# Where the fourth set of activation forms is made, ahead of the seven-product feed-forward

## The chip, the core and the metric

The kernel runs on one NeuronCore of a Trainium2 chip. The metric is the device time of one launch, in microseconds (us). The engines are named as the profile names them: PE is the matmul engine (PEld its weight loads), DVE the vector engine, ACT the scalar engine, POOL the general one, SP the queue from which nearly all loads are issued. Each engine takes its own instructions in the order of the program.

## The reference

A two-layer decoder trunk runs over 512 prompt rows and 32 sample rows (8 sequences of 4), together T = 544 columns of the activation matrix, 1024 features high. Each layer is half feed-forward, mixer, half feed-forward, gated embedding. The feed-forward is what matters here, and it runs four times:

```python
def rmsnorm(x, g):
    y = x * lax.rsqrt(jnp.mean(x * x, axis=-1, keepdims=True) + EPS)
    return y * g
def swiglu(x, w1, w3, w2):
    return (jax.nn.silu(x @ w1) * (x @ w3)) @ w2
# in layer i
h = h + 0.5 * swiglu(rmsnorm(h, ffn1_norm[i]), ffn1_w1[i], ffn1_w3[i], ffn1_w2[i])
h = h + mixer(rmsnorm(h, mix_norm[i]))          # layer 0: gMLP, layer 1: attention
h = h + 0.5 * swiglu(rmsnorm(h, ffn2_norm[i]), ffn2_w1[i], ffn2_w3[i], ffn2_w2[i])
```

All is in float32; the inner width of the feed-forward is 2816.

## The kernel before

**Layout.** Features lie on the 128 partitions, so the activations h are 8 chunks of 128 x 544. A float32 product is made of three matmuls of rounded halves: each operand is split into a high part (a rounded copy, on ACT) and a low part (source less high part, on DVE), and PE adds high x high, high x low and low x high. The 544 columns are taken as two halves of 272.

**Weights.** SP loads a block of 128 x 1024 (`_load`, L208). `_sum` makes a sum or difference of two blocks on DVE (L227), and `_split` the two parts of a piece (ACT cast L241, then DVE subtraction L242). `prepare` runs these a few pieces ahead of the piece that PE takes. All of them, the activations and the forms below live in one pool of 45 buffers named `big`, each 128 x 1088 floats.

**The feed-forward** (`ffn`) has three stretches. First `plain` pairs of inner blocks are made in the plain way: per pair four tiles (two blocks, w1 and w3), each 8 x 6 matmuls (`mm`, L285, L289, L291) with one copy out of PSUM on ACT (L471). The first feed-forward of layer 0 makes two pairs (eight plain tiles), the other three make one (four). Beside the first tile, ACT and DVE also make the norm's factor `rstd` (L385 to L403).

Then `ffn_steps` makes the remaining pairs by a scheme of Strassen's kind with seven products in place of eight (L538, 24 matmuls each; order 1, 5, 6, 2, 7, 3, 4), and puts tiles of the second matrix w2 (L285 to L291, added to h at L577) between them. Products 1, 6, 7 and 4 gather in one PSUM buffer, so what stands there is read out between them: ACT copies after 1, 5 and 6 (L546), DVE adds after 2 (L553), after 7 (L555) and after 3 (L557), and ACT copies after 4 (L560). Product 4 may not start before L555 has read the buffer. There are three PSUM buffers named `ps`: two hold the sums of the products and one the tile of w2, so the next tile of w2 may not start before L577 has read the last.

The gate of a finished pair (`gate`) is four steps: times `rstd` (DVE L496), Silu (ACT L499), product (DVE L502), split (L329, L330). One step of each open pair follows each product. In `ffn_steps` the order of PE, ACT, DVE and POOL is that in which the code is written; ahead of it a list scheduler places the instructions of each engine by its own rules.

**The forms.** Products 3, 5, 6, 7 and 4 need differences of the activations. Per pair of chunks `forms` makes one set: two scaled copies on ACT (L351), then on DVE

```python
nc.vector.tensor_tensor(two(t13), x[:, :, HT:], two(x[:, 0, :]), ALU.subtract)      # L355
self.split_pair(f13, t13)                                                           # ACT L329, DVE L330
nc.vector.tensor_tensor(t24[:, :HT], x[:, 1, HT:], t13[:, :HT], ALU.subtract)       # L357
nc.vector.tensor_tensor(t24[:, HT:], x[:, 1, :HT], t24[:, :HT], ALU.subtract)       # L358
self.split_pair(f24, t24)                                                           # ACT L329, DVE L330
```

So a set is four instructions of ACT, five of DVE and three `big` buffers (x, which is free after L358, and f13 and f24, which stay for the whole feed-forward). Four sets are needed. `box["f"]` holds those that the stage ahead has made: none ahead of the first feed-forward, three ahead of the second (the mixer of layer 0 makes sets 0, 1 and 2 as chunks 1, 3 and 5 are done), two ahead of the third and two ahead of the fourth. In `ffn` the rest is made beside the plain tiles by `more(n)`, which makes one set if fewer than n are there. With one pair and fewer than three sets (`lead`) it is called ahead of each tile; otherwise after each tile's copy, with a count that grows with the tile.

Of the kernel before, what the change touches and what calls it, by code (L numbers as in the profile page):

```python
# [51 lines left out]
NKP = NC_ // 2  # L52
# [50 lines left out]
def halves(x):  # L103

    return x.rearrange("p (a b) -> p a b", a=2)
# [27 lines left out]
def whole(p):  # L133

    return unwoven(span(p))


class Builder:
# [312 lines left out]
    def ffn(self, h, box, gcol, rstd, on_chunk, plain=1):  # L451

        nc, eng = self.nc, mybir.EngineType
        self.ahead = (2, 3, 6)
        first, xs, xf = [], self.pairs(box), box["f"]

        def more(n):
            if len(xf) < min(n, NKP):
                xf.append(self.forms(h, gcol, len(xf), xs))
        hid, todo = {}, ([], [])  # L460
        lead = plain == 1 and len(xf) < 3
        for f in range(2 * plain):
            g = self.big()
            for w in range(2):
                if lead:
                    more(len(xf) + 1)
                if rstd is None:
                    p, rstd = self.tile_rstd(xs, box["acc"])
                else:
                    p = self.tile_mm(xs)  # L470
                nc.scalar.copy(halves(g[:, w]), whole(p))  # L471
                for t in todo:
                    if t:
                        t.pop(0)()
                if not lead:
                    more((2 * f + w + 1) // plain)
            first.append((f // 2, f % 2, g))
            if f % 2 and f < 2 * plain - 1 or lead and f == 0:
                for j, a, g in first:
                    todo[a].extend(self.gate(hid, rstd, j, a, g))  # L480
                first = []
        assert self.chain is None
        for j, a, g in first:
            todo[a].extend(([None] * 3 if j == 0 else []) + self.gate(hid, rstd, j, a, g))
        with self.tc.manual_schedule(engines={eng.PE, eng.Activation, eng.DVE, eng.Pool}):
            self.ffn_steps(h, xf, rstd, hid, todo, plain, on_chunk)
        self.ahead = (2, 2, 4)
        self.pins = 2
        return rstd
# [1106 lines left out]
```

## Time and profile before

| what | us |
|---|---|
| median of three timed runs | 1931.98 (1931.47 to 1932.03) |
| the profiled execution, its own time | 1931.48 |
| its span | 1929.7 |
| first feed-forward: eight plain tiles end, products begin | 56.95 |
| second feed-forward: four plain tiles end, products begin | 528.80 |

Times of rows count from the start of the span; the profiled execution lasts 1.78 us longer than it. A row of the timeline gives the start, the length, the engine, the line and operation, the tiles (written <- read) and in brackets how long the engine sat idle ahead of it and what ended that. Rows of one kind that follow each other are merged (x48). An instruction's length reaches until its result is written, so the next on the same engine can start some 0.1 us before the length is over.

### The profile page before, as it was taken

Reading aid. Unit: us, or ns where it says so; the run is one execution under the profiler, and the core shown is the slowest. Engines: PE = TensorE matmul, PEld = TensorE weight load, DVE = VectorE, ACT = ScalarE, POOL = GpSimd, SP = SyncE. Lnnn points to the kernel's source line nnn. Section 1 sums busy time; section 2 is a strip of 40 time slices with the busy share of each in tenths; the row PEclk is TensorE's granted clock in tenths of the full one; section 3 lists DMA queues with packets and bytes.
Section 4 is the critical chain, followed back from the end, with each engine's and each line's share of the span. In section 5 each row is a group of like instructions: output and inputs, shape, how many; then the busy total and the mean of one; then the engine's idle time right before and its main releaser. Section 6 shows DMA issues by size and latency. Waiting matters only on the chain.

```text
span 1929.7 us, 39007 instructions
## 1 busy us (share of the span) xinstructions
PE 1906.5 (99%) x16508; PEld 1872.2 (97%) x16508; DVE 1457.5 (76%) x1799; ACT 950.2 (49%) x1396; POOL 142.6 (7%) x190
## 2 busy tenths in 40 slices
PE   9999999999999999999999999999999999999999
PEld 8999999999999999999999999999977899999999
DVE  7887877556788877766578887877476888878774
ACT  7544434424554444454466454444374754444461
POOL 0000000410100000023000000001131300000020
PEclk9999999999999999999999999999999999999999
DMA  5233234312223233431484232324769332332431
GB/s 195 79 112 121 84 123 147 108 48 88 88 88 107 86 120 105 153 104 45 144 306 157 103 129 69 129 86 136 217 210 341 101 110 81 112 113 86 139 109 47
DMA packets 98048, 237.62 MB, mean 123 GB/s; under 512 B 12130, under 2 KB 29826, under 8 KB 97874
## 3 DMA queue, kind: packets, MB, share of 16 engines
q1 hardware_dynamic: 97730, 235.09, 36.9%
q8 instruction: 130, 2.13, 0.5%
q14 instruction: 44, 0.36, 0.1%
q10 hardware_dynamic: 144, 0.04, 0.0%
HBM read 218.65 MB, written 16.44 MB: 122 GB/s over the span
## 4 chain that ended last, share of the span: by engine, by line
PE 89%; DVE 6%; ACT 3%; issue 1%; DMA 1%; POOL 0%; SPq 0%; ACTq 0%; DVEq 0%; POOLq 0%
PE ps L538 31%; PE ps L285 15%; PE ps L291 15%; PE ps L289 15%; PE pb L538 5%; DVE big L242 2%; ACT big L241 1%; DVE big L227 1%; DMA big<-in_cv 1%; PE ps L891 1%; PE ps L892 1%; PE ps L893 1%; DVE big L496 0%; DVE big L330 0%; PE ps L1285 0%
## 5 line engine op out<-in xcount | busy, mean ns | idle before, releaser
L538 PE MATMUL ps<-big,big 128*128 128x272 f32 x5616 | 668.8, 279 | 5.9 <-DVE big L555 3.5
L538 PEld LDWEIGHTS ps<-big,big 128*128 128x128 f32 x5616 | 658.5, 189 | 7.0 <-issue 4.0
L242 DVE TENSOR_TENSOR big<-big,big 128x1024 fp32r<-128x1024 f32 (+2 forms) x505 | 582.8, 1157 | 93.4 <-ACT big L241 92.9
L241 ACT CAST big<-big 128x1024 fp32r<-128x1024 f32 (+2 forms) x505 | 483.1, 977 | 326.5 <-DVE big L227 251.9
L285 PE MATMUL ps<-big,big 128*128 128x272 f32 x2668 | 531.3, 280 | 3.8 <-ACT big L241 2.3
L291 PE MATMUL ps<-big,big 128*128 128x272 f32 x2668 | 529.2, 280 | 1.8 <-DVE big L242 1.7
L289 PE MATMUL ps<-big,big 128*128 128x272 f32 x2668 | 528.3, 279 | 0.0
L285 PEld LDWEIGHTS ps<-big,big 128*128 128x128 f32 x2668 | 408.3, 189 | 8.5 <-ACT big L241 5.7
L291 PEld LDWEIGHTS ps<-big,big 128*128 128x128 f32 x2668 | 407.9, 189 | 3.6 <-DVE big L242 3.1
L289 PEld LDWEIGHTS ps<-big,big 128*128 128x128 f32 x2668 | 407.9, 189 | 0.0
L370 POOL TENSOR_TENSOR st<-st,tmp 128x544 f32<-128x544 f32 (+1 forms) x63 | 87.5, 1389 | 1476.7 <-ACT tmp L368 1476.5
L227 DVE TENSOR_TENSOR big<-big,big 128x1024 f32<-128x1024 f32 x156 | 190.2, 1219 | 0.0
L577 DVE SCALAR_TENSOR_TENSOR big<-ps,big 128x544 f32<-128x544 f32 x128 | 92.5, 723 | 104.0 <-PE ps L291 103.0
L546 ACT COPY tmp<-ps 128x544 f32<-128x544 f32 x117 | 71.6, 612 | 107.5 <-PE ps L538 107.2
L496 DVE TENSOR_TENSOR big<-big,st 128x1088 f32<-128x1088 f32 x88 | 113.2, 1289 | 3.3 <-ACT big L560 2.0
L538 PE MATMUL pb<-big,big 128*128 128x272 f32 x936 | 114.8, 279 | 0.0
L538 PEld LDWEIGHTS pb<-big,big 128*128 128x128 f32 x936 | 111.3, 189 | 0.0
L499 ACT ACTIVATE big<-big 128x544 f32<-128x544 f32 x88 | 58.0, 660 | 88.1 <-DVE big L496 88.0
L341 ACT ACTIVATE big<-big,gains 128x544 fp32r<-128x544 f32 (+1 forms) x80 | 55.3, 703 | 90.3 <-DVE big L577 55.0
L330 DVE TENSOR_TENSOR big<-big,big 128x544 fp32r<-128x544 f32 (+1 forms) x112 | 79.4, 715 | 22.8 <-ACT big L329 22.6
L342 DVE SCALAR_TENSOR_TENSOR big<-big,gains,big 128x544 fp32r<-128x544 f32 (+1 forms) x80 | 64.6, 817 | 23.4 <-ACT big L341 23.4
L329 ACT CAST big<-big 128x544 fp32r<-128x544 f32 (+1 forms) x112 | 71.2, 644 | 11.9 <-DVE big L502 7.5
(218 smaller groups left out, 1388.5 us busy)
## 6 DMA issues: line engine op xcount, KB each, us to landing
big<-in_w SPq DMA_DIRECT2D x156, 512.0 KB
big<-in_w2b SPq DMA_DIRECT2D x96, 384.0 KB
big<-in_w13p SPq DMA_DIRECT2D x16, 512.0 KB
big<-in_w2a SPq DMA_DIRECT2D x16, 512.0 KB
big<-in_win SPq DMA_DIRECT2D x16, 512.0 KB
big<-in_wg SPq DMA_DIRECT2D x16, 512.0 KB
big<-in_ck SPq DMA_DIRECT2D x16, 512.0 KB
big<-in_cv SPq DMA_DIRECT2D x16, 512.0 KB
```

The lines of the kernel that those rows point to most:

```text
L227: self.nc.vector.tensor_tensor(t, a, b, ALU.add if op == "+" else ALU.subtract)
L241: self.nc.scalar.copy(hi, src)
L242: self.nc.vector.tensor_tensor(lo, src, hi.bitcast(F32), ALU.subtract)
L285: i = nc.tensor.matmul(o, wh, xh[:, b], start=s, stop=False)
L289: nc.tensor.matmul(o, wh, xl[:, b], start=False, stop=False)
L291: nc.tensor.matmul(o, wl, xh[:, b], start=False, stop=e)
L330: self.nc.vector.tensor_tensor(pair[:, 1, cols], src, pair[:, 0, cols].bitcast(F32), ALU.subtract)
L370: nc.gpsimd.tensor_tensor(acc[:, cols], acc[:, cols], sq, ALU.add)
L496: tt(g, g, rstd.unsqueeze(1).broadcast_to([P, 2, T]), ALU.mult)
L538: nc.tensor.matmul(turns(dst[w]), a[:, c], woven(b), start=k in "152" and kp == 0 and n == 0, stop=kp == NKP - 1 and n == 2, skip_group_ch ...
L546: nc.scalar.copy(t["r" + k], t["C" if k == "5" else "A"])
L577: nc.vector.scalar_tensor_tensor(halves(h[c]), whole(out), 0.5, halves(h[c]), ALU.mult, ALU.add)
```

## The change

One line of `ffn`, the call after each plain tile:

```diff
                 if not lead:
-                    more((2 * f + w + 1) // plain)
+                    more((2 * f + w + 1) // plain if len(xf) < 3 else NKP)
```

NKP is 4. Where three sets are there, the call asks for all four, so the fourth is made after the tile at which it stands. This touches two places. In the second feed-forward three sets are there from the start: the fourth was made after plain tile 4 and is now made after tile 1. In the first feed-forward (two pairs, counts 0, 1, 1, 2, 2, 3, 3, 4) the third set comes with tile 6, so the fourth is made after tile 7 where it was made after tile 8. The third and fourth feed-forward take the other branch (`lead`) and keep their order. PE's, POOL's and SP's instructions keep theirs as well; on SP some loads go to other buffers of the pool and so wait for other instructions.

Second feed-forward, DVE. L392 ends the norm's factor beside the first plain tile; L242 and L227 are low parts and sums of weights; L355 to L330 are the fourth set. Before, the set stands behind the low part for product 5 and the sum for product 6, ahead of the low parts for products 6 and 2 (the last two rows):

```order
L392 SCALAR_TENSOR_TENSOR st_6042<-tmp_6043,st_6042 128x544
L227 TENSOR_TENSOR big_6122<-big_6057,big_6059 128x1024
L242 TENSOR_TENSOR big_6175<-big_6122,big_6174 128x1024
L227 TENSOR_TENSOR big_6178<-big_6122,big_5987 128x1024
L355 TENSOR_TENSOR tmp_6233<-big_6230 128x544
L357 TENSOR_TENSOR tmp_6234<-big_6230,tmp_6233 128x272
L358 TENSOR_TENSOR tmp_6234<-big_6230,tmp_6234 128x272
L330 TENSOR_TENSOR big_6235<-tmp_6233,big_6235 128x544
L330 TENSOR_TENSOR big_6236<-tmp_6234,big_6236 128x544
L242 TENSOR_TENSOR big_6272<-big_6178,big_6271 128x1024
L242 TENSOR_TENSOR big_6276<-big_6061,big_6275 128x1024
```

With the change it stands among the steps of the norm's factor, ahead of the low part of the fourth plain tile's weights (the last row):

```order
L403 TENSOR_TENSOR tmp_6033<-st_5502,tmp_6032 128x544
L355 TENSOR_TENSOR tmp_6056<-big_6053 128x544
L357 TENSOR_TENSOR tmp_6057<-big_6053,tmp_6056 128x272
L388 SCALAR_TENSOR_TENSOR tmp_6043<-st_6042 128x544
L358 TENSOR_TENSOR tmp_6057<-big_6053,tmp_6057 128x272
L330 TENSOR_TENSOR big_6058<-tmp_6056,big_6058 128x544
L391 SCALAR_TENSOR_TENSOR tmp_6043<-pb_6036,tmp_6043 128x272
L391 SCALAR_TENSOR_TENSOR tmp_6043<-pb_6037,tmp_6043 128x272
L330 TENSOR_TENSOR big_6059<-tmp_6057,big_6059 128x544
L392 SCALAR_TENSOR_TENSOR st_6042<-tmp_6043,st_6042 128x544
L242 TENSOR_TENSOR big_6068<-big_5924,big_6067 128x1024
```

and behind the sum for product 6 (second L227 of the next piece) the low parts for products 6 and 2 come at once:

```order
L242 TENSOR_TENSOR big_6133<-big_5987,big_6132 128x1024
L227 TENSOR_TENSOR big_6136<-big_6071,big_6073 128x1024
L242 TENSOR_TENSOR big_6189<-big_6136,big_6188 128x1024
L227 TENSOR_TENSOR big_6192<-big_6136,big_5987 128x1024
L242 TENSOR_TENSOR big_6272<-big_6192,big_6271 128x1024
L242 TENSOR_TENSOR big_6276<-big_6075,big_6275 128x1024
```

The five instructions of DVE moved up by six to nine places.

Second feed-forward, ACT. L471 are the copies of the four plain tiles, L351 and L329 the fourth set, L241 high parts of weights, L546 the first copies out of the products. Before:

```order
L241 CAST big_6118<-big_5987 128x1024
L471 COPY big_5982<-ps_6067 128x544
L471 COPY big_6117<-ps_6124 128x544
L241 CAST big_6174<-big_6122 128x1024
L351 ACTIVATE big_6230<-big_95,gains 128x544 x2
L329 CAST big_6235<-tmp_6233 128x544
L471 COPY big_6117<-ps_6180 128x544
L329 CAST big_6236<-tmp_6234 128x544
L241 CAST big_6271<-big_6178 128x1024
L241 CAST big_6275<-big_6061 128x1024
L546 COPY tmp_6308<-ps_6246 128x544
```

With the change, from the copy of the first plain tile on:

```order
L471 COPY big_5982<-ps_5989 128x544
L351 ACTIVATE big_6053<-big_95,gains 128x544 x2
L385 ACTIVATE st_6042<-pb_6036,eps 128x272
L385 ACTIVATE st_6042<-pb_6037,eps 128x272
L329 CAST big_6058<-tmp_6056 128x544
L329 CAST big_6059<-tmp_6057 128x544
L241 CAST big_6067<-big_5924 128x1024
L471 COPY big_5982<-ps_6081 128x544
L241 CAST big_6132<-big_5987 128x1024
L471 COPY big_6131<-ps_6138 128x544
L241 CAST big_6188<-big_6136 128x1024
L241 CAST big_6271<-big_6192 128x1024
```

The four instructions of the set moved to behind the first L471; the cast of the fourth plain tile's weights (first L241 of the piece) stands behind them, that of product 1's weights behind the second L471, and those for products 6 and 2 ahead of the last L471.

First feed-forward, ACT, from the copy of plain tile 7 to the first copy out of the products. Before:

```order
L471 COPY big_592<-ps_601 128x544
L241 CAST big_653<-big_597 128x1024
L329 CAST big_709<-big_175 128x544
L329 CAST big_712<-big_328 128x544
L351 ACTIVATE big_715<-big_95,gains 128x544 x2
L471 COPY big_592<-ps_659 128x544
L329 CAST big_720<-tmp_718 128x544
L329 CAST big_721<-tmp_719 128x544
L241 CAST big_758<-big_657 128x1024
L241 CAST big_762<-big_524 128x1024
L546 COPY tmp_791<-ps_731 128x544
```

With the change:

```order
L471 COPY big_592<-ps_601 128x544
L351 ACTIVATE big_653<-big_95,gains 128x544 x2
L329 CAST big_658<-tmp_656 128x544
L329 CAST big_659<-tmp_657 128x544
L241 CAST big_667<-big_597 128x1024
L329 CAST big_723<-big_175 128x544
L329 CAST big_726<-big_328 128x544
L471 COPY big_592<-ps_673 128x544
L241 CAST big_758<-big_671 128x1024
L241 CAST big_762<-big_524 128x1024
L546 COPY tmp_791<-ps_731 128x544
```

The set now stands ahead of the cast for product 5 (first L241) and ahead of the copy of tile 8 (second L471), where it stood behind both. On DVE it moved in the same way: from behind the low part for product 5, the sum for product 6 and the splits of the first gated pair to ahead of them.

## The prediction

> **What bounds the kernel now.** I read the page's busy times first, then its chain, then PE's waits.
>
> ```profile
> span 1929.7 us, 39007 instructions
> PE 1906.5 (99%) x16508; PEld 1872.2 (97%) x16508; DVE 1457.5 (76%) x1799; ACT 950.2 (49%) x1396; POOL 142.6 (7%) x190
> PE 89%; DVE 6%; ACT 3%; issue 1%; DMA 1%; POOL 0%; SPq 0%; ACTq 0%; DVEq 0%; POOLq 0%
> ```
>
> PE works 1906.5 of 1929.7 us and holds 89% of the chain; the change leaves its work alone. So the change can win only from the 23.2 us in which PE stands still, and it can lose only by making PE wait anew. PE's waits by releaser:
>
> ```profile
> PE ps L538 <- DVE big L555: 3.5, 3, 2.1
> PE ps L538 <- ACT tmp L546: 2.4, 3, 1.3
> PE ps L285 <- DVE big L577: 1.4, 2, 0.7
> ```
>
> The first three numbers of the list are the total, the count and the longest. Which of them lie in the two feed-forwards that the change touches, the timeline of PE shows. Second feed-forward:
>
> ```profile
> 528.80 8.50 PE L538 MATMUL ps<-big,big 128*128 128x272 f32 x72
> 537.14 2.94 PE L538 MATMUL pb<-big,big 128*128 128x272 f32 x24
> 539.92 5.72 PE L538 MATMUL ps<-big,big 128*128 128x272 f32 x48
> 547.79 11.36 PE L538 MATMUL ps<-big,big 128*128 128x272 f32 x96 [2.14 <-DVE big L555]
> ...
> 564.54 2.94 PE L538 MATMUL ps<-big,big 128*128 128x272 f32 x24
> ...
> 568.22 0.47 PE L285 MATMUL ps<-big,big 128*128 128x272 f32 x2 [0.74 <-DVE big L577]
> ```
>
> These are products 1, 5, 6, then 2, then 7 and 3, then 4 and the next pair's. One product takes 539.92 - 537.14 = 2.78 us. Products 7 and 3 would let product 4 begin at 539.92 + 5.56 = 545.48; it begins at 547.79, so 2.31 us are lost (the row says 2.14, since it counts from the modelled end). Likewise 568.22 - 564.54 - 2.78 = 0.90 us are lost at L577. First feed-forward:
>
> ```profile
> 56.95 5.72 PE L538 MATMUL ps<-big,big 128*128 128x272 f32 x48
> 63.32 3.05 PE L538 MATMUL ps<-big,big 128*128 128x272 f32 x24 [0.64 <-ACT tmp L546]
> ...
> 71.76 2.94 PE L538 MATMUL ps<-big,big 128*128 128x272 f32 x24
> 75.34 0.47 PE L285 MATMUL ps<-big,big 128*128 128x272 f32 x2 [0.63 <-DVE big L577]
> ```
>
> Lost: 63.32 - 62.51 = 0.81 us ahead of product 6, and 75.34 - 74.54 = 0.80 us at L577. The four together are 4.82 us; this is all that the change can reach.
>
> **The change, second feed-forward.** DVE around the fourth set:
>
> ```profile
> 525.09 1.23 DVE L242 TENSOR_TENSOR big<-big,big 128x1024 fp32r<-128x1024 f32 x1 [5.92 <-ACT big L241]
> 526.23 1.22 DVE L227 TENSOR_TENSOR big<-big,big 128x1024 f32<-128x1024 f32 x1
> 527.37 0.72 DVE L355 TENSOR_TENSOR tmp<-big 128x544 f32<-128x544 f32 x1
> ...
> 531.14 2.36 DVE L242 TENSOR_TENSOR big<-big,big 128x1024 fp32r<-128x1024 f32 x2 [0.22 <-ACT big L241]
> 533.41 1.22 DVE L227 TENSOR_TENSOR big<-big,big 128x1024 f32<-128x1024 f32 x1
> 535.75 1.23 DVE L242 TENSOR_TENSOR big<-big,big 128x1024 fp32r<-128x1024 f32 x1 [1.11 <-ACT big L241]
> ...
> 539.28 1.23 DVE L242 TENSOR_TENSOR big<-big,big 128x1024 fp32r<-128x1024 f32 x1 [1.17 <-ACT big L241]
> 540.42 2.49 DVE L496 TENSOR_TENSOR big<-big,st 128x1088 f32<-128x1088 f32 x2
> ...
> 543.96 0.78 DVE L553 TENSOR_TENSOR big<-pb,tmp 128x272 f32<-128x272 f32 x2
> 544.65 1.22 DVE L242 TENSOR_TENSOR big<-big,big 128x1024 fp32r<-128x1024 f32 x1
> ...
> 546.92 0.72 DVE L555 TENSOR_TENSOR big<-ps,tmp 128x544 f32<-128x544 f32 x1
> ...
> 567.36 0.72 DVE L577 SCALAR_TENSOR_TENSOR big<-ps,big 128x544 f32<-128x544 f32 x1
> ```
>
> The set costs DVE 531.14 - 527.37 = 3.77 us, with its own waits, just as the products begin. From there to L555 DVE never waits for PE: it is late by itself, and L555, whose product 7 was done at 539.92 + 2.78 = 542.70, runs at 546.92. With the change the set falls into the 5.92 us in which DVE had nothing to do (up to 525.09). That idle time is its cover. The weights of plain tile 4 then stand behind it. A plain tile has 48 pairs of matmuls like two products, so 5.56 us; tile 1 ends near 528.80 - 3 x 5.56 = 512.1, its copy takes 0.6, the two scaled copies of the set 1.4 (an estimate from the copy's length), the set on DVE 3.8, the last steps of the norm's factor between them up to 2 (four of the same size), the low part of the tile's weights 1.2: done between 519.1 and 521.1, and I take 519.8, since ACT and DVE overlap. Tile 4 begins at 528.80 - 5.56 = 523.24. So 2.1 to 4.1 us of cover are left; each us beyond that would cost one.
>
> What is late next? The chain sum L227, ACT cast, low part L242 takes 535.75 - 533.41 = 2.34 us. ACT's rows matter now too:
>
> ```profile
> 529.00 0.61 ACT L471 COPY big<-ps 128x544 f32<-128x544 f32 x1 [0.23 <-PE ps L291]
> ...
> 538.20 1.05 ACT L241 CAST big<-big 128x1024 fp32r<-128x1024 f32 x1 [1.97 <-DVE big L227]
> 539.15 0.61 ACT L546 COPY tmp<-ps 128x544 f32<-128x544 f32 x1
> ...
> 542.02 0.66 ACT L499 ACTIVATE big<-big 128x544 f32<-128x544 f32 x1
> 542.94 0.66 ACT L499 ACTIVATE big<-big 128x544 f32<-128x544 f32 x1 [0.26 <-DVE big L496]
> 543.50 1.03 ACT L241 CAST big<-big 128x1024 fp32r<-128x1024 f32 x1
> ```
>
> - Low parts for 6 and 2: 526.23 + 2.34 = 528.57 (was 531.14). Sum for 7: + 2.27 (533.41 - 531.14) = 530.84.
> - Its cast now finds ACT at the copy after product 1. A copy starts 0.20 us after PE's next work does (529.00 against 528.80), so at 531.78; the cast follows 0.50 later (539.15 to about 539.65) at 532.28, its low part 1.08 later (538.20 to 539.28) at 533.36, the sum for 3 at 534.50 (1.14 later, as 539.28 to 540.42), its low part at 536.84, L496 at 537.98, L553 at 541.52 (3.54 later).
> - ACT's copy after product 6 cannot precede 537.14 + 0.20 = 537.34 (was 539.15). From it to the cast at 543.50 are 4.35 us, less 0.36 by which the second L499 was held (542.02 to 542.94 is 0.92, the next pitch 0.56): 541.33. Its low part comes at 542.41, later than DVE would be ready (541.52 + 0.69), so ACT decides: 2.24 us ahead of 544.65.
> - L555 follows 2.27 later, at 544.68, and PE 0.87 after it (546.92 to 547.79), at 545.55. Of the 2.31 us, 0.07 remain.
>
> Between L555 and L577 DVE runs without a wait for PE, so L577 also comes 2.24 earlier and PE's start there moves from 568.22 to 565.98. **Second feed-forward: 2.24 us.** Later PE and DVE go on with the same distance as before.
>
> **First feed-forward.**
>
> ```profile
> 51.59 0.61 ACT L471 COPY big<-ps 128x544 f32<-128x544 f32 x1 [2.00 <-PE ps L291]
> ...
> 62.66 0.60 ACT L546 COPY tmp<-ps 128x544 f32<-128x544 f32 x1
> ```
>
> ```profile
> 65.52 1.22 DVE L227 TENSOR_TENSOR big<-big,big 128x1024 f32<-128x1024 f32 x1
> ...
> 74.47 0.72 DVE L577 SCALAR_TENSOR_TENSOR big<-ps,big 128x544 f32<-128x544 f32 x1
> ```
>
> Here DVE has no large gap and the set moves by one tile. ACT makes the scaled copies behind the copy at 51.59 (0.5 and 1.4, until 53.5), DVE the set in about 3.4 (3.77 above, of which a part was waiting for ACT) until 56.9, then the low part for 5 (1.14; product 5 needs it at 56.95 + 2.78 = 59.73, so 1.7 us of cover) and the sum for 6, done at 59.2. ACT then casts twice (1.0 each) and copies at 61.2, where it stood at 62.66: before, both casts stood behind the set's last split. PE starts 0.66 after that copy (62.66 to 63.32), so it could at 61.9, ahead of 62.51: the 0.81 us go. What is late next is the low part for product 6, which I get done at 62.8, when PE wants it at 62.51 + 0.46; up to 0.2 us may remain. Behind ACT's copy (0.5) stand two Silus (0.56 each) and a cast whose low part follows 1.08 later, at 63.9; it is of half size (0.6), so the sum at 65.52 comes at 64.48. From there to L577 it is DVE with ACT, not PE: L577 comes 1.04 earlier and PE from 75.34 to 74.30. **First feed-forward: 1.04 us**, whatever remains at product 6, since L577 decides.
>
> **The sum** is 3.3 us: 1931.48 - 3.3 = 1928.2 for the profiled execution, and 1928.7 against the median of 1931.98, which lies 0.5 above it. Unknown are the new waits of loads and the places where I put an instruction between rows. Their bounds are 4.82 us won (all four waits gone: 1927.2) and, below, the case in which the waits only move.
>
> [...] The change takes two lasting buffers some 14 us sooner, so loads behind it get other buffers. The three loads of the next blocks, and the answer on who waited for a load between 485 and 600:
>
> ```profile
> 500.49 1.28 SPq L208 DMA_DIRECT2D big<-in_w  x3
> ```
>
> ```profile
>   ACT big L241: 0.2, 1
> ```
>
> They were issued from 500.49 on; they now wait for buffers that PE reads up to the first three k-steps of the mixer's last tile, 0.7 us apart, so they go some 1 us later. The sum that reads the first two stands at about 520.9. From issue to use there are 19 us, and nothing but 0.2 us ever waited for a load here. I take 0 and keep 0.2 us as the other end. [...]
>
> **The rivals.**
>
> *All four waits go*: if DVE comes 1 us earlier still at both L577, PE never waits there: 4.8 us, 1927.2. For it speaks that DVE's waits for ACT shrink; against, that the copy after product 6 cannot precede PE.
>
> *The waits move*: L555 comes early, but a copy after a product (L546) or L577 holds PE in its place, in one feed-forward or both. The three waits for L546 of up to 1.3 us show that this happens. About half is given back: 1.0 to 2.0 us won, 1930.0 to 1931.0.
>
> *Slower*: DVE and ACT take the set in order, so a load that lands late would hold the sum at 520.9 and all that stands behind. It decides once that sum begins later than 525.09 - 2.34 = 522.75: then the low part at 525.09 is late, and so is L555. From there each us takes one from the win of 3.3, and slower by 0.2% needs a landing near 530: 1936. The 19 us speak against it.
>
> *It does nothing*: were the gap up to 525.09 filled by other work first, the set would end as late as now: 1932. The order shows the set ahead of the second copy, so this is unlikely.
>
> **How the numbers follow.** The forecast has 0.60, all four gone 0.19, the waits move 0.14, slower 0.04, nothing 0.03. Predicted is 1928.7. The range goes from 1927.2 to 1931.0, which leaves out little but the last two cases. A time counts as faster from 0.2% on, 3.86 us below 1931.98, about what a measurement of this kernel can tell from no change: that is under 1928.1. The forecast lies 0.6 us above that bound; 0.08 of its 0.60 may fall below. With the 0.19 that makes faster 0.27; slower is 0.04 and within 0.2% the other 0.69.
>
> **What would show it.** In the profile of the changed kernel DVE should have L355 near 514 and no set behind 526; L555 should stand near 544.7 less the 1.0 that the first feed-forward gives, the wait ahead of product 4 should be under 0.3, the wait for L546 ahead of the first feed-forward's product 6 gone, and both waits for L577 still there with 0.5 to 0.8 us lost. I am wrong if L555 still holds PE by over 0.5 us, if PE waits for a low part (L242) in the plain tiles, or if a sum (L227) waits for a load.

## The result, and the profile after

| | before | changed |
|---|---|---|
| median of 14 runs each, on one chip, us | 1931.34 (1930.51 to 1932.29) | 1927.2 (1926.71 to 1928.32) |
| ratio, 95% interval | | 0.998 (0.9973 to 0.9987) |
| the profiled execution, its own time | 1931.48 | 1928.06 |
| its span | 1929.7 | 1926.3 |

The change makes the kernel 4.1 us faster (1931.34 - 1927.2; by the interval 2.5 to 5.2). The page of the changed kernel, its first lines and the chain:

```profile
span 1926.3 us, 39008 instructions
PE 1904.8 (99%) x16508; PEld 1869.8 (97%) x16508; DVE 1457.4 (76%) x1799; ACT 949.2 (49%) x1396; POOL 143.4 (7%) x190
PE 89%; DVE 5%; ACT 2%; DMA 2%; issue 1%; SPq 0%; POOL 0%; ACTq 0%; DVEq 0%
```

Each engine listed has as many instructions as before, and PE's share of the chain is the same. The waits of PE (total, count, longest) show where the time went:

```profile
PE ps L538 <- ACT tmp L546: 1.7, 2, 1.3
PE ps L538 <- DVE big L555: 1.4, 2, 1.0
PE ps L285 <- DVE big L577: 1.2, 2, 0.7
```

Of three waits for L555 the one of 2.1 us is gone (3.5 to 1.4), of three for L546 one of 0.7 (2.4 to 1.7); both for L577 are still there. PE's timeline, first feed-forward and then second:

```profile
56.21 8.55 PE L538 MATMUL ps<-big,big 128*128 128x272 f32 x72
64.60 2.94 PE L538 MATMUL pb<-big,big 128*128 128x272 f32 x24
70.16 2.94 PE L538 MATMUL ps<-big,big 128*128 128x272 f32 x24
73.59 0.47 PE L285 MATMUL ps<-big,big 128*128 128x272 f32 x2 [0.48 <-DVE big L577]
...
527.05 8.50 PE L538 MATMUL ps<-big,big 128*128 128x272 f32 x72
535.39 2.94 PE L538 MATMUL pb<-big,big 128*128 128x272 f32 x24
538.17 16.96 PE L538 MATMUL ps<-big,big 128*128 128x272 f32 x144
...
560.53 2.94 PE L538 MATMUL ps<-big,big 128*128 128x272 f32 x24
564.20 0.47 PE L285 MATMUL ps<-big,big 128*128 128x272 f32 x2 [0.73 <-DVE big L577]
```

Products 1, 5 and 6 of the first feed-forward now run as one row (x72), and so do products 7, 3, 4 and the next pair's first three in the second (x144): nothing holds PE inside. To compare kernels I take two stretches, each from the start of product 1 to PE's start behind the first L577. The first went from 75.34 - 56.95 = 18.39 to 73.59 - 56.21 = 17.38 us, the second from 568.22 - 528.80 = 39.42 to 564.20 - 527.05 = 37.15 us. That is 1.01 + 2.27 = 3.28 us. Between them lie 453.46 us in both kernels (528.80 - 75.34 and 527.05 - 73.59). DVE in the second feed-forward:

```profile
512.09 0.72 DVE L355 TENSOR_TENSOR tmp<-big 128x544 f32<-128x544 f32 x1 [2.22 <-ACT big L351]
...
516.79 2.36 DVE L242 TENSOR_TENSOR big<-big,big 128x1024 fp32r<-128x1024 f32 x2
519.07 1.22 DVE L227 TENSOR_TENSOR big<-big,big 128x1024 f32<-128x1024 f32 x1
523.28 1.23 DVE L242 TENSOR_TENSOR big<-big,big 128x1024 fp32r<-128x1024 f32 x1 [2.99 <-ACT big L241]
524.42 1.22 DVE L227 TENSOR_TENSOR big<-big,big 128x1024 f32<-128x1024 f32 x1
526.75 2.36 DVE L242 TENSOR_TENSOR big<-big,big 128x1024 fp32r<-128x1024 f32 x2 [1.11 <-ACT big L241]
...
542.91 0.72 DVE L555 TENSOR_TENSOR big<-ps,tmp 128x544 f32<-128x544 f32 x1
```

The set stands at 512.09, its idle stretch has shrunk from 5.92 to 2.99 us, and behind the sum at 524.42 there is no L355 any more.

### The profile page after: what moved, and what is told of

Read it like the earlier page. It is cut to its first block, busy times and chain, and to the rows that moved or that the text cites. A ratio compares the mean times of both kernels' runs of the same rounds, so it can differ in the third digit from the quotient of the medians.

```text
span 1926.3 us, 39008 instructions
## 1 busy us (share of the span) xinstructions
PE 1904.8 (99%) x16508; PEld 1869.8 (97%) x16508; DVE 1457.4 (76%) x1799; ACT 949.2 (49%) x1396; POOL 143.4 (7%) x190
## 4 chain that ended last, share of the span: by engine, by line
PE 89%; DVE 5%; ACT 2%; DMA 2%; issue 1%; SPq 0%; POOL 0%; ACTq 0%; DVEq 0%
PE ps L538 31%; PE ps L285 15%; PE ps L291 15%; PE ps L289 15%; PE pb L538 5%; DVE big L242 1%; DMA tmp<-rows 1%; ACT big L241 1%; PE ps L891 1%; PE ps L892 1%; PE ps L893 1%; DVE big L227 1%; DVE big L330 0%; PE ps L1285 0%; PE ps L676 0%
## 5 line engine op out<-in xcount | busy, mean ns | idle before, releaser
L242 DVE TENSOR_TENSOR big<-big,big 128x1024 fp32r<-128x1024 f32 (+2 forms) x505 | 582.1, 1156 | 86.7 <-ACT big L241 85.9
L241 ACT CAST big<-big 128x1024 fp32r<-128x1024 f32 (+2 forms) x505 | 482.4, 975 | 325.1 <-DVE big L227 251.5
L227 DVE TENSOR_TENSOR big<-big,big 128x1024 f32<-128x1024 f32 x156 | 190.1, 1219 | 0.0
L577 DVE SCALAR_TENSOR_TENSOR big<-ps,big 128x544 f32<-128x544 f32 x128 | 92.5, 722 | 104.1 <-PE ps L291 103.2
L546 ACT COPY tmp<-ps 128x544 f32<-128x544 f32 x117 | 71.5, 611 | 111.3 <-PE ps L538 111.3
L330 DVE TENSOR_TENSOR big<-big,big 128x544 fp32r<-128x544 f32 (+1 forms) x112 | 79.3, 714 | 22.7 <-ACT big L329 22.5
L329 ACT CAST big<-big 128x544 fp32r<-128x544 f32 (+1 forms) x112 | 71.2, 643 | 12.2 <-DVE big L502 7.4
```

Source lines behind the costliest of these rows:

```text
L227: self.nc.vector.tensor_tensor(t, a, b, ALU.add if op == "+" else ALU.subtract)
L241: self.nc.scalar.copy(hi, src)
L242: self.nc.vector.tensor_tensor(lo, src, hi.bitcast(F32), ALU.subtract)
L330: self.nc.vector.tensor_tensor(pair[:, 1, cols], src, pair[:, 0, cols].bitcast(F32), ALU.subtract)
L546: nc.scalar.copy(t["r" + k], t["C" if k == "5" else "A"])
L577: nc.vector.scalar_tensor_tensor(halves(h[c]), whole(out), 0.5, halves(h[c]), ALU.mult, ALU.add)
```

## The experiments

The theory: the set of forms costs the path what DVE and ACT spend on it, if it stands beside the products, and nothing if it falls into DVE's idle stretch. The rivals: the buffers and loads that move with it are what counts; each tile sooner gives its share; part of the cost has only moved. All edits are to the line of the change, except in the last one.

**Each feed-forward alone.** First the second one:

```diff
-                    more((2 * f + w + 1) // plain if len(xf) < 3 else NKP)
+                    more((2 * f + w + 1) // plain if len(xf) < 3 or plain == 2 else NKP)
```

> Only the second feed-forward has its fourth set after plain tile 1; the first keeps the order of before. I measure two stretches: S1, from the start of product 1 of the first feed-forward to PE's start behind the first L577 (before 75.34 - 56.95 = 18.39 us, after 73.59 - 56.21 = 17.38), and S2, the same in the second (before 568.22 - 528.80 = 39.42, after 564.20 - 527.05 = 37.15). Theory (each place pays by itself, because DVE's queue is shorter by one set when the products begin): S1 18.39, S2 37.15, both within 0.1, and the time 2.3 us below before. Rival (the second place only pays because the first moved the buffers of the pool): S2 stays at 39.4. Rival (the rest of the measured 4.1 us comes from the start of the program, where product 1 began 0.74 us sooner): the products begin at 56.2 here too, though the order up to there is that of before; by the theory that start only varies from run to run.

and then the first one (`or plain == 1`):

> Only the first feed-forward has its fourth set one tile sooner; the second keeps the order of before. Theory: S1 17.38 and S2 39.42, both within 0.1, the time 1.0 us below before. Rival (PE's wait for L577 there would have shrunk by itself): S1 18.4. If both parts were worth half of 4.1, the time would be 2.0 below before.

Measured: with the second alone 1927.49 us against 1930.93 (ratio 0.9983, 0.9974 to 0.9992), stretches 73.89 - 55.44 = 18.45 and 564.52 - 527.36 = 37.16. With the first alone 1929.69 us against 1930.93 (0.9993, 0.9984 to 1.0002), stretches 73.21 - 55.81 = 17.40 and 566.08 - 526.66 = 39.42. Each half gives its own stretch what the whole change gives it and leaves the other as before. The interval of the first alone takes in 1, so its gain is read from the stretch. By the stretches the two gains are independent, and the second feed-forward carries two thirds. The times fell by more than was expected of them: 1930.93 - 1927.49 = 3.44 us with the second alone, where 2.3 was expected, and 1.24 us with the first alone, where 1.0 was.

**The set one and two tiles later** (second feed-forward, first as with the change; `f + w > 0` and `f > 0`):

```diff
-                    more((2 * f + w + 1) // plain if len(xf) < 3 else NKP)
+                    more((2 * f + w + 1) // plain if len(xf) < 3 else NKP if plain == 2 or f > 0 else 0)
```

> The fourth set of the second feed-forward is made with plain tile 2, one tile later than the change makes it; the first feed-forward is as with the change. Theory (all that counts is whether the set falls into the stretch in which DVE has nothing to do, which ends when the low part of the weights for product 1 is due): the set still falls into it, so 37.15 us from product 1's start to PE's start behind the first L577, within 0.2, and no wait of PE for L555 over 0.3. Rival (each tile later gives back its share of the 3.4 us between the placings with tile 1 and with tile 3): 38 to 39 us, with a wait for L555 between 0.8 and 1.5.

> The second feed-forward makes its fourth set after plain tile 3 (after: tile 1, before: tile 4). In the order of instructions the set then stands two places sooner on DVE than before: ahead of the low part for product 5 and the sum for product 6, still behind DVE's idle stretch. Theory (what pays is that the set falls into that idle stretch, not that it is sooner): the set starts when the copy of tile 3 is done, and now also the low part for 5 and the sum for 6 wait for it; by the rows of before the low parts for 6 and 2 come at about 532.2 where they came at 531.1, so S2 is 40.4 (40.1 to 40.7), 1.0 longer than before. Rival (sooner is better, in proportion): a third of the way from before to after, S2 38.7.

Measured: with tile 2, 564.19 - 527.04 = 37.15 us (one run of 1928.57), no wait for L555. With tile 3, 567.09 - 526.56 = 40.53 us (one run of 1929.58), which is 1.1 us worse than with tile 4. DVE and PE with tile 3:

```profile
523.19 0.73 DVE L355 TENSOR_TENSOR tmp<-big 128x544 f32<-128x544 f32 x1 [6.26 <-ACT big L351]
...
526.53 1.23 DVE L242 TENSOR_TENSOR big<-big,big 128x1024 fp32r<-128x1024 f32 x1 [0.22 <-ACT big L241]
```

```profile
538.68 5.83 PE L538 MATMUL ps<-big,big 128*128 128x272 f32 x48 [0.83 <-ACT tmp L546]
546.66 11.36 PE L538 MATMUL ps<-big,big 128*128 128x272 f32 x96 [2.15 <-DVE big L555]
```

DVE stands idle for 6.26 us and only then takes the set, since the scaled copies wait for the tile's copy; the low part for product 5, ahead of the set before, now stands behind it at 526.53. So one tile sooner than before is worse, two sooner is as good as three. It is no share per tile: what counts is on which side of the idle stretch the set stands in DVE's queue.

**The set made twice**, at the new place and, unused, at the old one:

```diff
-                    more((2 * f + w + 1) // plain if len(xf) < 3 else NKP)
+                    more((2 * f + w + 1) // plain if len(xf) < 3 else NKP); gcol == G_FFN2 and f == w == 1 and self.forms(h, gcol, NKP - 1, xs)
```

> As after, but in the second feed-forward a second copy of the fourth set is made after plain tile 4, where the set stood before; nobody reads it. Theory (the cost is DVE's time in that place, 3.8 us): S2 is back at 39.4 (39.2 to 39.6), with PE waiting 2.1 us for L555 ahead of product 4. Rival (what paid is that the set is ready sooner, or that buffers and loads moved): S2 stays at 37.2.

Measured: 566.11 - 526.70 = 39.41 us, PE waiting 2.14 us for L555 again (one run of 1929.95):

```profile
545.68 11.36 PE L538 MATMUL ps<-big,big 128*128 128x272 f32 x96 [2.14 <-DVE big L555]
```

The forms that are used, with the buffers they hold, are early here as with the change; only the work at the old place is back, and with it the whole 2.26 us (39.41 - 37.15). So the gain is the time of DVE and ACT taken from there. And since the stretch is that of before (39.42) although the buffers are held early, the early hold costs it nothing.

**No set at the new place:**

```diff
-                    more((2 * f + w + 1) // plain if len(xf) < 3 else NKP)
+                    xf.append(xf[2]) if gcol == G_FFN2 and len(xf) == 3 else more((2 * f + w + 1) // plain if len(xf) < 3 else NKP)
```

> From the change as it is, the fourth set of forms of the second feed-forward is left out: its third set is used in its place, so a quarter of the first products of that feed-forward is computed from the wrong columns; the matmuls, loads and splits of weights are all still there. Theory (the set is wholly hidden where the change puts it): from the start of product 1 to PE's start behind the first L577 of the second feed-forward stay 37.15 us, within 0.1, and the span stays within 1 us of the changed kernel's. Rival (the set still holds DVE or ACT back at its new place): the stretch becomes shorter, by up to the 0.73 us that PE still waits for L577, so 36.4. First feed-forward: 17.38 us as with the change.

Measured: 73.20 - 55.82 = 17.38 and 563.81 - 526.66 = 37.15 us; one run of 1927.85. DVE's idle stretch is back at its old length:

```profile
522.94 1.23 DVE L242 TENSOR_TENSOR big<-big,big 128x1024 fp32r<-128x1024 f32 x1 [5.92 <-ACT big L241]
```

The third set stands in for the fourth here, so the work of the fourth is left out. Without it the stretch is not one hundredth shorter: what is made with the first tile is free.

**The first feed-forward's sets with tiles 1 to 4**, beside the changed kernel once more on the same chip:

```diff
-                    more((2 * f + w + 1) // plain if len(xf) < 3 else NKP)
+                    more(2 * f + w + 1 if len(xf) < 3 else NKP)
```

> The four sets of the first feed-forward are made with plain tiles 1, 2, 3 and 4 of its eight instead of 2, 4, 6 and 7; the second feed-forward is as with the change. Theory (PE's last wait for L577 in the first feed-forward is DVE's delay from the set that still stands beside the first products): L577 comes at least 0.65 us sooner, PE's wait there goes, and the stretch from product 1's start to PE's start behind it is 16.7 us (17.38 less 0.65), so some 0.7 us less in all, if nothing new is late in the plain tiles. Rival (the wait for L577 is that of the chain matmul, Silu, split and L577 itself, not of the set): the stretch stays at 17.3 to 17.4. Third: the sets stand ahead of the splits of the plain tiles' weights, PE waits for L242 there, and product 1 itself begins later, by up to the 3.4 us of one set.

> The changed kernel itself, on the same chip as the run beside it: 1927.2 us within 0.8; 17.38 and 37.15 us for the two stretches. What differs between its profile and the earlier one of the same kernel, in the start of the program and in the stretch behind the second feed-forward, shows how far a single profiled span can be read; by the four kernels so far that are alike there, up to 1.5 us at each place.

Measured: 1931.17 us (0.9999 of before, 0.999 to 1.0008) beside 1927.17 us for the changed kernel (0.998, 0.997 to 0.9989): 4.0 us are lost. The theory came, and so did the third case, though not as it was told: product 1 begins later by more than its bound of 3.4 us, and PE waits longest for a cast on ACT (L241), not for a low part (L242). PE no longer waits for L577, and the first stretch is 78.03 - 61.35 = 16.68 us, 0.70 less than 17.38. But product 1 starts at 61.35 where the changed kernel beside it has 56.02. PE's timeline in the plain tiles:

```profile
32.62 0.40 PE L291 MATMUL ps<-big,big 128*128 128x272 f32 x2
36.55 0.50 PE L285 MATMUL ps<-big,big 128*128 128x272 f32 x2 [3.54 <-ACT big L241]
...
38.44 0.66 PE L289 MATMUL ps<-big,big 128*128 128x272 f32 x2
38.89 0.66 PE L291 MATMUL ps<-big,big 128*128 128x272 f32 x2
...
41.61 0.44 PE L291 MATMUL ps<-big,big 128*128 128x272 f32 x2
41.89 0.40 PE L285 MATMUL ps<-big,big 128*128 128x272 f32 x2
```

and ACT's cast for this tile, in the changed kernel and then here:

```profile
31.89 1.04 ACT L241 CAST big<-big 128x1024 fp32r<-128x1024 f32 x1
32.94 1.28 ACT L499 ACT_TABLE_LOAD   x1
```

```profile
33.06 1.28 ACT L499 ACT_TABLE_LOAD   x1 [1.59 <-DVE big L496]
34.36 0.66 ACT L499 ACTIVATE big<-big 128x544 f32<-128x544 f32 x1
34.92 0.63 ACT L329 CAST big<-tmp 128x544 fp32r<-128x544 f32 x1
35.45 1.04 ACT L241 CAST big<-big 128x1024 fp32r<-128x1024 f32 x1
```

The cast that stood ahead of the first gate's table load now stands behind it, behind the Silu and behind a split of the second set, 3.56 us later (35.45 - 31.89), and PE waits 3.54 us for it. A second loss follows: from 38.44 to 41.61 seven pairs of matmuls take 3.17 us, 0.45 each in place of 0.23 (from 78.50 to 79.42, four pairs take 0.92), so another 7 x 0.45 - 7 x 0.23 = 1.5 us. Pause and slow stretch are 5.0 of the 5.33 us.

**The first L577 ahead of the low part in front of it**, in the loop of `ffn_steps`, with the change kept:

```diff
+        sooner = [lambda: after[0]()]
         for n, (kind, at, k, part) in enumerate(self.ffn_slots(plain)):
             now, after = after, []
             (products if kind == "g" else second)(at, k, part)
             for f in now:
                 f()
+            if sooner and kind == "w" and after:
+                sooner.pop()()
+                after = []
```

> The changed kernel with one exchange on DVE in each feed-forward: the first update L577 is issued ahead of the low part L242 that stood in front of it (562.19 and 563.34 in the second feed-forward of the changed kernel), not behind it. Theory (the two waits of PE for L577 that the change left are DVE's order, not the set of forms and not the matmuls that feed L577): L577 starts about 1.6 us sooner, right behind L553, PE does not wait for it, and PE starts behind it at the end of the product before: 17.38 - 0.65 = 16.73 us in the first feed-forward and 37.15 - 0.89 = 36.26 us in the second, 1.5 us less in all, near 1925.7 us. Rival (the low part that now comes second, or an operation behind it, is late instead): PE's wait for L577 goes but one for L242 or L555 of the same size takes its place within the next 10 us, and the program's time stays at 1927.2.

Measured: 1925.05 us against 1931.15 (ratio 0.9967, 0.9955 to 0.9979), stretches 73.41 - 56.66 = 16.75 and 563.06 - 526.80 = 36.26 us. DVE and PE there:

```profile
560.75 0.78 DVE L553 TENSOR_TENSOR big<-pb,tmp 128x272 f32<-128x272 f32 x2
561.46 0.71 DVE L577 SCALAR_TENSOR_TENSOR big<-ps,big 128x544 f32<-128x544 f32 x1
562.10 1.81 DVE L242 TENSOR_TENSOR big<-big,big 128x1024 fp32r<-128x1024 f32 x2
```

```profile
560.28 2.94 PE L538 MATMUL ps<-big,big 128*128 128x272 f32 x24
563.06 0.39 PE L285 MATMUL ps<-big,big 128*128 128x272 f32 x2
565.84 2.94 PE L538 MATMUL ps<-big,big 128*128 128x272 f32 x24
```

L577 runs where DVE would have waited 0.41 us for ACT. The low part behind it starts 0.16 us later, counted from product 1 (562.10 - 526.80 against 562.19 - 527.05), PE waits for none of that, and PE goes from product to tile without a wait (563.06 - 560.28 is the 2.78 of a product). Both stretches together are 53.01 us, against 54.53 with the change alone and 57.81 before. It is faster than before by its time; that it is faster than the changed kernel is read from the stretches, as the two did not run side by side.

## Why the prediction was right

The forecast case came: L555 and the first feed-forward's L546 stop holding PE, and both L577 still do. Its sum was 2.24 + 1.04 = 3.28 us; the stretches gave 2.27 + 1.01. Point by point, counted from the start of product 1 in each kernel (528.80 and 56.95 in the prediction, 527.05 and 56.21 measured):

| step | predicted | measured |
|---|---|---|
| low parts for 6 and 2 | -0.23 | 526.75, -0.30 |
| cast for 7, behind the copy after product 1 | 3.48 | 530.54, 3.49 |
| copy after product 6, not sooner than PE allows | 8.54 | 535.59, 8.54 |
| cast ahead of L555, where ACT decides | 12.53 | 539.57, 12.52 |
| L555 | 15.88 | 542.91, 15.86 |
| PE behind L577, second | 37.18 | 564.20, 37.15 |
| first feed-forward: copy that held product 6 | 4.25 | 60.45, 4.24 |
| first feed-forward: sum behind it | 7.53 | 63.78, 7.57 |
| PE behind L577, first | 17.35 | 73.59, 17.38 |

The measured starts of ACT and of the sum are these rows of the changed kernel:

```profile
60.45 0.60 ACT L546 COPY tmp<-ps 128x544 f32<-128x544 f32 x1
...
530.54 1.05 ACT L241 CAST big<-big 128x1024 fp32r<-128x1024 f32 x1
...
535.59 0.61 ACT L546 COPY tmp<-ps 128x544 f32<-128x544 f32 x1 [0.47 <-PE ps L538]
...
539.57 1.03 ACT L241 CAST big<-big 128x1024 fp32r<-128x1024 f32 x1
```

```profile
63.78 1.22 DVE L227 TENSOR_TENSOR big<-big,big 128x1024 f32<-128x1024 f32 x1
```

- *The cover.* Tile 4's weights were taken as done at 519.8. The row at 516.79 merges two low parts, tile 4's and behind it product 1's. The first takes 1.22 us and is done at 518.01; as product 1 starts 1.75 us sooner than before (527.05 against 528.80), that is 519.76 on the clock of before, just what was taken. Tile 4 began at 527.05 - 5.56 = 521.49, so 3.5 us of cover were left, inside the 2.1 to 4.1. That nothing was paid there the kernel without the set shows.
- *The loads.* 0 was taken, and 0 it was: no engine waited for a load in this part, and the set made twice shows that buffers held early do not take from the gain.
- *The buffers.* Two of PE's four waits vanished with the change, and the other two went when one instruction of DVE was moved, with no byte of room more. So they came from the order in the queues of DVE and ACT, as their releasers said.
- *The rivals.* "All four waits go" did not come, though its time did: 1927.2. With the last experiment it came, and the stretches then gave 57.81 - 53.01 = 4.80 us where 4.8 was worked out. "The waits move" did not come with the change; with tile 3 the set brings a wait of 0.83 for L546, so the mechanism exists.
- *The size.* Predicted 1928.7, measured 1927.2. Of these 1.5 us, 0.64 are the median of before, 1931.98 in three runs and 1931.34 in fourteen. The other 0.9 is the difference between 3.28 us in the stretches and 4.1 in the medians, inside the interval of 2.5 to 5.2. The range held the time only at its lower end, 1927.2, and that was luck: it had no term for the scatter of the medians. Its chances put 0.69 on a time within 0.2% of the one before and 0.27 on faster; 4.1 us is 0.21%, just on the faster side, and the interval reaches to both. What was worked out a little wrong is the loss left at the second L577: 564.20 - 560.53 - 2.78 = 0.89 us, where 0.5 to 0.8 was named.
- *The signs.* L355 was to stand near 514 and stands at 512.09, 513.84 on the clock of before. PE does not wait ahead of product 4, and no sum waits for a load. L555 was to stand near 543.7 and stands at 542.91, in a profile in which the first product 1 starts 0.74 us sooner. PE does wait for low parts in the plain tiles of the first feed-forward, but at 34.33 at the latest, ahead of all that the change moves; that longest wait, 0.62 us, was there before (0.61 ahead of 35.07).

Open is whether anything outside the two feed-forwards belongs to the change. The profiled spans differ by 3.4 us, of which 3.28 lie in the stretches; the start of the program and what follows scatter by more than the rest (next section but one). But the times lie further from those of before than the stretches say: by 4.14 against 3.28 us here, by 3.44 against 2.26 with the second feed-forward alone, by 6.10 against 4.80 with L577 moved. A part of this goes with the granted clock (same section), and the rest is not explained.

## What to carry to other kernels

Work that is due at some later point belongs ahead of an idle stretch of the engine that must do it, in that engine's queue. Where exactly made no difference here (tiles 1 and 2, 37.15 us with each), but one tile later it stood behind the stretch and cost more than at its old place (40.53 against 39.42 us). So look in the timeline for the idle time ahead of the step that is late, and follow which queue places fall on which side of it. Count what a moved step has in front of and behind it on every engine that it uses; ahead of tiles whose weights were just in time, sets made sooner cost PE 5 us here. When a wait is left, read the two instructions of the releaser's engine in front of the one that is late: one of them may be in no hurry.

## What the runs showed of the hardware

*Behind a pause of 3.54 us PE ran at half its pace.* In the kernel with the sets at tiles 1 to 4 the granted clock was lower behind the pause of 3.54 us. The windows of 36 to 42 us, first of the changed kernel and then of the one with the sets at tiles 1 to 4 (busy time of PE, PEld, DVE, ACT and POOL, then PEclk, DMA share and GB/s):

```profile
36.00:42.00 6.00, 6.00 (x54) 6.00 (x54) 5.52 (x8) 4.18 (x8) 1.38 (x1) 1.00 0.48 176
```

```profile
36.00:42.00 6.00, 4.92 (x25) 4.72 (x26) 5.30 (x8) 4.16 (x8) 0.71 (x1) 0.72 0.37 124
```

The clock is 0.72 there and 1.00 in the other, and a pair of matmuls took twice its time for 3.2 us. In the windows on either side in the same trace, 24 to 36 and 42 to 50 us, the clock is 1.00. The slow pairs did not come at once: PE started again at 36.55, and the first of them is at 38.44, 1.89 us later. The trace shows pairs of that length once more, five in the 2.27 us from 8.57 to 10.84, 0.45 each, where the longest wait of PE in the span so far was 1.62 us. So no single pause of 3.5 us is needed for them. The clock of the first 80 us is 0.96, and the window of 36 to 42 us alone would make it 0.98 ((80 - 6 x 0.28) / 80), so it was below 1.00 elsewhere in them too. What ends a slow stretch no run shows.

That the pause brought the later of the two stretches fits the runs: in all eleven executions of this kernel the mean granted clock is below 1.000 (0.997 to 0.999), with the changed kernel beside it in two of eleven. Behind the pauses of 2.14 us ahead of product 4 there is no such stretch: with only the first feed-forward changed, 96 matmuls from 545.65 on took 11.19 us, 0.117 each, and 24 before them 2.78, 0.116 each.

*One profiled span can't be read to the microsecond.* In the ten profiles without the sets at tiles 1 to 4, product 1 of the first feed-forward started between 55.44 and 56.95 us, and in all eleven the way from PE's start behind the second feed-forward's L577 to the end of the span took 1360.6 to 1362.6. The same kernel, profiled twice, has 56.21 and 56.02 at the start and 1362.1 and 1361.4 at the end. The two stretches of it agree to 0.01 us, which is why the experiments were read by them. With the second feed-forward alone changed, product 1 of the first began at 55.44 us, though the order up to there is that of before (56.95): so that start says nothing of the change.

PE's pace near the start differs between profiles too: in the profile of before a pair of matmuls took 0.45 us from 9.43 to 13.51, in that of the changed kernel 0.23 from 9.37 to 10.99. The windows list a clock of 1.00 for both, so why the pairs were slow there is not shown. The times of the executions of before go with the granted clock. On the chip where the changed kernel ran again, 9 of 21 executions of before have a mean granted clock of 1.000, with a median of 1930.69 us (the other 12 have 1931.40), and 9 of 11 of the changed kernel, with 1927.17: 3.52 us apart, where all of them are 3.94 apart and the stretches 3.28. Why the lower clock is rarer with the change no run shows; with the second feed-forward alone changed it is as rare (10 of 11 at 1.000).
